# Attention between dense matmuls, loads on another queue, and pooling moved behind the dense stage

## The chip, the cores and the metric

The kernel runs on one core of a Trainium2 chip. The metric is the time of one execution on the device in microseconds (us), as the median of several runs. The core's engines work at the same time, each through its own list of instructions in order: TensorE (PE) multiplies matrices, VectorE (DVE) and ScalarE (ACT) work elementwise, GpSimd (POOL) and SyncE (SP) here mostly issue DMA transfers. An instruction may wait for another engine or for a transfer; what stands behind it on its engine then waits too.

## The reference

One transformer-like block on 2048 positions of width 1024, in float32:

```python
u = _rmsnorm(h, norm_mix_g[l])
z = jnp.einsum('bsd,dn->bsn', u, w_in[l])
q, k, v, pz, ga, gp = jnp.split(z, offs, axis=-1)
a = _attention_branch(q, k, v)                 # 3 groups of 4 heads, dilations 1, 4, 16
p = _pool_branch(pz, w_pool_grp[l], pool_scale[l])   # trailing means over 2, 4, 8, 16
merged = (jax.nn.sigmoid(ga) * jnp.einsum('bsc,cd->bsd', a, w_att_out[l])
          + jax.nn.sigmoid(gp) * jnp.einsum('bsc,cd->bsd', p, w_pool_out[l]))
h = h + jnp.einsum('bsd,de->bse', merged, w_out[l])
m = _rmsnorm(h, norm_mlp_g[l])
hid = jnp.square(jax.nn.relu(jnp.einsum('bsd,df->bsf', m, w_mlp_in[l])))
h = h + jnp.einsum('bsf,fd->bsd', hid, w_mlp_out[l])
return _rmsnorm(h, norm_final_g)
```

Attention looks back over 128 strided positions, softmax with a distance penalty; the three groups' results are weighted by their softmax denominators.

## The kernel before

The sequence is worked on in two halves of 1024 positions (hf 0 and 1), each as two tiles of 512 (t). Positions lie along the free axis, channels on the 128 partitions.

**Normalisation** (normed_x). For each t the eight tiles of x are loaded on SP's queue, squared on ACT, and the squares added on DVE (L277, seven adds per t). A matmul with a matrix of ones (L124, tile xst) sums over the partitions; ACT and DVE make the factor 1/rms from it, DVE multiplies x by it (L285). Seven left-hand combinations of the scaled tiles (B11, T1, T2, B22, T3, B21, T4; combine) are each split into a high and a low part: a cast on ACT (L141), a subtraction on DVE (L142).

**Dense stage** (stage). Per half there are 20 pairs of output blocks: nine for q, k, v, three for the pooling input (pz), eight for the gates (g). Two pairs are worked side by side in each of ten rounds. A pair takes seven steps in the order A11, S1, S2, S4, S3, A12, A22, a block form of multiplication with seven products; each step is 12 matmuls of 128x512 into a PSUM bank with the tag "b" or "c" (L148 to L150). The weights are loaded on SP's queue, summed on DVE (L291 to L294) and split (L141, L142). The results go through DVE or ACT (total, L308 to L312) and are stored from POOL's queue. A half has 1680 of these matmuls.

**Hook.** After each round j a hook issues a share of the half's attention blocks (32 in half 1, 64 in half 2; the share is 5 or 8) and at j = 6, 7, 8 four pooling blocks each. At j = 8 the first half also issues the second half's normalisation and the second half the group weights.

**Attention block** (attention). It loads q, k and v (SP), multiplies q by k for two heads (tiles s0, s1; L458), adds the penalty on DVE (L460), takes the row maximum (L462), the exponentials on ACT (L464), transposes the scores on PE (tile t, L468), copies them (L470), multiplies by v (tile o, L474), copies the result (L476) and stores it from POOL's queue (L477). A block reads one or two blocks of keys.

**Pooling block** (pooling). It loads a 128x528 piece of pz (SP), adds shifted copies on DVE (L422), subtracts the token (L428; L431 and L432 mend the first 16 positions) and stores it to p_d from POOL's queue.

**Group weights** transpose the row maxima and sums (row_s, row_t), form the three groups' weights and store them (wts_d). **merge** loads the pooled tiles (p), the attention results (o) and the weights (wb), combines and splits them, and multiplies by w_pool_out (z_pp) and w_att_out (z_pq); the gates follow. Behind it come w_out (z_o) and the MLP.

Eight PSUM banks are shared out: three "b", two "c", s0, s1, and "t" for transposes, attention results, sums of squares. In SBUF the temporaries tt, hx and h22 have four buffers each: the scores sb and their transposes pt share tt, q and k lie in hx, v and the result in h22.

A scheduler sets the order of the instructions on each engine from the program's order and its own estimate of time, so that neighbours in the code need not be neighbours on an engine.

Of the kernel before, what the change touches and what calls it, by code (L numbers as in the profile page):

```python
# [9 lines left out]
F32 = mybir.dt.float32  # L10
# [7 lines left out]
P = 128  # L18
D = 1024
KD = D // P  # L20
SEQ = 2048
C = 512
# [25 lines left out]
def trunk_kernel(ctx: ExitStack, tc, xt, w_qk, w_v, w_pz, w_grp, w_gates, w_att, w_pool, w_o, w_1, w_2, cols, out):  # L48
    nc = tc.nc
# [71 lines left out]
    def ssq_to_rstd(pool, ps, ssq, dst, key, tags, bufs):  # L121

        n = ssq.shape[-1]
        nc.tensor.matmul(ps, ones, ssq, start=True, stop=True)  # L124
        y = pool.tile([P, C], F32, name=f"y_{key}", tag=tags[0], bufs=bufs)[:, :n]
        nc.scalar.activation(y, ps, AF.Ln, scale=1.0 / D, bias=eps)
        nc.scalar.activation(y, y, AF.Exp, scale=-0.5)
        v = pool.tile([P, C], F32, name=f"var_{key}", tag=tags[1], bufs=bufs)[:, :n]
        nc.vector.tensor_scalar(v, ps, 1.0 / D, EPS, op0=ALU.mult, op1=ALU.add)
        t = pool.tile([P, C], F32, name=f"t_{key}", tag=tags[2], bufs=bufs)[:, :n]  # L130
        nc.vector.tensor_mul(t, y, y)
        nc.vector.tensor_mul(t, t, v)
        nc.vector.tensor_scalar(t, t, -0.5, 1.5, op0=ALU.mult, op1=ALU.add)
        nc.vector.tensor_mul(dst, y, t)
# [18 lines left out]
    psd = pool_of(pds, "psd", space=PSUM)  # L153
    banks = {"pool": psd, "b": 3, "c": 2}

# [41 lines left out]
    wp = pool_of(wps, "wp")  # L197
# [5 lines left out]
    def wtile(name, tag="zz", bufs=ZB):  # L203
        return wp.tile([P, C], F32, name=name, tag=tag, bufs=bufs)
# [51 lines left out]
    def normed_x(hf):  # L256

        got = {}
        ssq = [wtile(f"xss_{hf}_{t}", "ssq", 2) for t in range(2)]

        def load(k, t, tag):
# [3 lines left out]

        for t in range(2):
            for k in range(KD):
                tag = {(0, 0): "tt", (1, 0): "hx", (1, 1): "h22", (0, 1): "zz"}[t, k // KH]
                x = load(k, t, tag)
                if tag != "zz":  # L270
                    got[k, t] = x
                if k == 0:
                    nc.scalar.square(ssq[t], x)
                else:
                    sq = wtile(f"xsq_{hf}_{k}_{t}")
                    nc.scalar.square(sq, x)
                    nc.vector.tensor_add(ssq[t], ssq[t], sq)  # L277
            ps = psd.tile([P, C], F32, name=f"xst_{hf}_{t}", tag="t")
            ssq_to_rstd(wp, ps, ssq[t], ssq[t], f"x{hf}_{t}", ("zz",) * 3, ZB)

        def piece(k, t, tag):
# [4 lines left out]
            return x  # L286
        return combine(piece, f"u{hf}")

# [122 lines left out]
    def pooling(c, n):  # L411

        key = f"{c}_{n}"
        z = temp(f"pz_{key}", "hx", TW)
        nc.sync.dma_start(z, pz_d[n, :, c * C:c * C + TW])
        wmax = max(w for _, _, w in POOL_SEGS[n])
# [18 lines left out]
    def attention(g, r, blk, hp):  # L435
# [4 lines left out]
        own, ks = slice(blk * P, (blk + 1) * P), slice((blk + 1 - nb) * P, (blk + 1) * P)  # L440
        qk = temp(f"qk_{key}", "hx", 3 * P)
        q, k = qk[:, :P], qk[:, P:P + W]
        nc.sync.dma_start(q, qk_d[g][hp, :, r, own])
        nc.sync.dma_start(k, qk_d[g][2 + hp, :, r, ks])
        vo = temp(f"vo_{key}", "h22", 3 * P)
        v, o = vo[:, P:P + W].rearrange("p (b f) -> p b f", b=nb), vo[:, :P]
        nc.sync.dma_start(v, v_d[g].rearrange("(i r) f -> r i f", r=d)[r, ks, hp * P:(hp + 1) * P]
                          .rearrange("(b p) f -> p b f", p=P))
# [17 lines left out]
        for par in range(2):  # L466
            for b in range(nb):
                nc.tensor.transpose(ps_t[:, par, b * P:(b + 1) * P], s[:, par, b * P:(b + 1) * P], ident)  # L468
        pt = temp(f"pt_{key}", "tt").rearrange("p (h j) -> p h j", h=2)[:, :, :W]
        nc.scalar.copy(pt, ps_t[:, :, :W])  # L470
        ps_o = psd.tile([P, C], F32, name=f"o_{key}", tag="t")[:, :P]
        for b in range(nb):
# [40 lines left out]

    next_inputs = [normed_x(0)]
    for hf in range(2):
        order = (1, 0, 2) if hf == 0 else (2, 1, 0)
# [10 lines left out]
        queue = [b for g in order for b in work[g]]  # L527
        share = -(-len(queue) // (7 if hf == 0 else 8))

        def hook(j):  # L530
            if j:
                for _ in range(min(share, len(queue))):
                    attention(*queue.pop(0))
            if j in (6, 7, 8):
                for n in (2 * j - 12, 2 * j - 11):
                    for t in range(2):
                        pooling(2 * hf + t, n)
            if j == 8:
                if hf == 0:
                    next_inputs.append(normed_x(1))  # L540
                else:
                    group_weights()
        stage(pairs, next_inputs[hf], hook)
    pds.close()
# [7 lines left out]
    def merge(hf):  # L552
# [10 lines left out]
        for t in range(2):  # L563
            c = 2 * hf + t
            for hp in range(2):
                a = None
                for g, d in enumerate(DIL):
                    o = temp(f"o_{c}_{g}_{hp}", "hx")
                    nc.sync.dma_start(o.rearrange("p (r i) -> p r i", r=d),
                                      o_d[g][hp, :, :, c * C // d:(c + 1) * C // d])  # L570
                    wb = wtile(f"wb_{c}_{g}_{hp}")
# [303 lines left out]
```

## Time and profile before

| what | value |
|---|---|
| median of 3 runs | 2937.55 us (2935.2 to 2938.49) |
| the profiled execution | 2930.1 us, its span 2928.3 us |
| PE busy | 2647.8 us (90%) |
| DVE busy | 1834.1 us (63%) |
| ACT busy | 1364.7 us (47%) |
| POOL busy | 384.2 us (13%) |
| mean granted PE clock | 0.933 of full speed (2.4 GHz) |

A busy share is an average over stages; the two dense halves with attention take the first 1200 us of the span, the merge follows up to about 1440, then w_out and the MLP. The granted clock stands at one of two levels, 1.2 or 2.4 GHz, and a mean between them says for how much of a stretch each held.

### The profile page before, as it was taken

Reading aid. Unit: us, or ns where it says so; the run is one execution under the profiler, and the core shown is the slowest. Engines: PE = TensorE matmul, PEld = TensorE weight load, DVE = VectorE, ACT = ScalarE, POOL = GpSimd, SP = SyncE. Lnnn points to the kernel's source line nnn. Section 1 sums busy time; section 2 is a strip of 40 time slices with the busy share of each in tenths; the row PEclk is TensorE's granted clock in tenths of the full one; section 3 lists DMA queues with packets and bytes.
Section 4 is the critical chain, followed back from the end, with each engine's and each line's share of the span. In section 5 each row is a group of like instructions: output and inputs, shape, how many; then the busy total and the mean of one; then the engine's idle time right before and its main releaser. Section 6 shows DMA issues by size and latency. Waiting matters only on the chain.

```text
span 2928.3 us, 35991 instructions
## 1 busy us (share of the span) xinstructions
PE 2647.8 (90%) x11838; PEld 2098.6 (72%) x11838; DVE 1834.1 (63%) x3031; ACT 1364.7 (47%) x2651; POOL 384.2 (13%) x667
## 2 busy tenths in 40 slices
PE   4799999289999998687899899989999899999996
PEld 4677777177767774466687688878887788878885
DVE  4854546784444455675798755586665584687557
ACT  3434443343444443332465555565555444464444
POOL 2012111011111111111011221112222000000000
PEclk7899999599989995788999999999999999999998
DMA  5234434243334344598766654445555946683433
GB/s 181 82 120 129 133 111 156 103 128 115 117 95 139 106 152 142 137 252 218 238 223 225 244 182 177 172 142 184 187 187 197 327 119 198 206 267 108 126 112 126
DMA packets 262475, 480.29 MB, mean 164 GB/s; under 512 B 57664, under 2 KB 108704, under 8 KB 262288
## 3 DMA queue, kind: packets, MB, share of 16 engines
q1 hardware_dynamic: 204592, 328.82, 35.9%
q0 software_dynamic: 57696, 149.17, 14.9%
q8 instruction: 93, 1.52, 0.2%
q14 instruction: 94, 0.77, 0.1%
HBM read 326.65 MB, written 151.14 MB: 163 GB/s over the span
## 4 chain that ended last, share of the span: by engine, by line
PE 60%; issue 21%; DVE 7%; DMA 6%; POOL 4%; ACT 1%; SPq 0%; POOLq 0%; DVEq 0%; ACTq 0%
PE z L149 6%; PE z L150 6%; PE z L148 6%; PE z_c_b L148 4%; PE z_c_b L150 4%; PE z_c_b L149 4%; PE z_c_c L150 3%; PE z_c_c L149 3%; PE z_c_c L148 3%; DMA x<-hid_d 1%; PE z_qk_b L148 1%; PE z_qk_b L149 1%; PE z_qk_b L150 1%; PE s L458 1%; PE z_qk_c L149 1%
## 5 line engine op out<-in xcount | busy, mean ns | idle before, releaser
L142 DVE TENSOR_TENSOR wl_S<-r_S,wh_S 128x512 fp32r<-128x512 f32 x128 | 88.3, 690 | 123.5 <-ACT wh_S L141 123.5
L141 ACT CAST wh_S<-r_S 128x512 fp32r<-128x512 f32 x128 | 79.9, 624 | 182.1 <-PE z L149 162.5
L149 PE MATMUL z<-xl_T,wh_S 128*128 128x512 f32 x384 | 149.6, 390 | 2.8 <-DVE xl_T L142 2.8
L150 PE MATMUL z<-xh_T,wl_S 128*128 128x512 f32 x384 | 149.4, 389 | 0.0
L142 DVE TENSOR_TENSOR wl_c_S<-s_c,wh_c_S 128x512 fp32r<-128x512 f32 x128 | 87.8, 689 | 97.4 <-ACT wh_c_S L141 97.1
L148 PE MATMUL z<-xh_T,wh_S 128*128 128x512 f32 x384 | 135.7, 389 | 0.0
L141 ACT CAST wh_c_S<-s_c 128x512 fp32r<-128x512 f32 x128 | 77.5, 619 | 98.0 <-PE z_c_b L149 48.1
L142 DVE TENSOR_TENSOR wl_g_S<-s_g,wh_g_S 128x512 fp32r<-128x512 f32 x64 | 44.2, 692 | 107.0 <-ACT wh_g_S L141 104.4
L141 ACT CAST wh_A<-r_A 128x512 fp32r<-128x512 f32 x96 | 59.6, 621 | 107.9 <-PE z L149 75.9
L464 ACT ACTIVATE sb<-sb,negm 128x256 f32<-128x256 f32 (+1 forms) x192 | 87.3, 458 | 45.0 <-DVE negm L462 44.8
L458 PE MATMUL s<-qk 64*128 64x256 f32 (+1 forms) x384 | 100.3, 442 | 7.9 <-DMA qk<-qk_d 4.7
L142 DVE TENSOR_TENSOR wl_A<-r_A,wh_A 128x512 fp32r<-128x512 f32 x96 | 66.1, 688 | 64.9 <-ACT wh_A L141 64.0
L477 POOL DMA_DIRECT2D o_d<-vo x96 | 52.0, 542 | 403.2 <-ACT vo L476 402.8
L149 PE MATMUL z<-xl_B,wh_A 128*128 128x512 f32 x256 | 101.1, 395 | 0.9 <-DVE xl_B L142 0.9
L148 PE MATMUL z<-xh_B,wh_A 128*128 128x512 f32 x256 | 94.6, 401 | 6.0 <-ACT xh_B L141 6.0
L150 PE MATMUL z<-xh_B,wl_A 128*128 128x512 f32 x256 | 99.9, 393 | 0.0
L460 DVE SCALAR_TENSOR_TENSOR sb<-steps,s 128x256 f32<-128x256 f32 (+1 forms) x192 | 62.8, 358 | 54.1 <-PE s L458 54.0
L470 ACT COPY pt<-t 128x512 f32<-128x512 f32 (+1 forms) x96 | 47.4, 493 | 91.9 <-PE t L468 91.9
L141 ACT CAST wh_c_A<-r_c 128x512 fp32r<-128x512 f32 x96 | 59.5, 620 | 65.1 <-PE z_c_c L149 31.1
L745 POOL TENSOR_TENSOR y<-y,frs 128x256 f32<-128x256 f32 x4 | 3.2, 811 | 656.5 <-ACT fsq L730 648.9
L149 PEld LDWEIGHTS z<-xl_T,wh_S 128*128 128x128 f32 x384 | 72.1, 188 | 18.6 <-DVE xl_T L142 3.7
L150 PEld LDWEIGHTS z<-xh_T,wl_S 128*128 128x128 f32 x384 | 72.1, 188 | 14.9
(659 smaller groups left out, 8490.7 us busy)
## 6 DMA issues: line engine op xcount, KB each, us to landing
x<-hid_d SPq DMA_DIRECT2D x160, 256.0 KB, 4.5
r_c<-in_w SPq DMA_DIRECT2D x64, 512.0 KB, 6.1
r_S<-w2s_d SPq DMA_DIRECT2D x128, 256.0 KB, 2.6
r_A<-in_w SPq DMA_DIRECT2D x96, 256.0 KB, 3.7
r_g<-in_w_gates SPq DMA_DIRECT2D x32, 512.0 KB, 3.9
r_w<-in_w SPq DMA_DIRECT2D x32, 512.0 KB, 3.2
w2s_d<-s_w POOLq DMA_DIRECT2D x64, 256.0 KB, 5.0
hid_d<-zS_c POOLq DMA_DIRECT2D x64, 256.0 KB, 3.6
```

Source lines behind the costliest of these rows:

```text
L141: nc.scalar.copy(hi, src)
L142: nc.vector.tensor_sub(lo, src, hi.bitcast(F32))
L148: nc.tensor.matmul(ps, lh, rh, start=start and i == 0, stop=False, skip_group_check=True)
L149: nc.tensor.matmul(ps, lh, rl, start=False, stop=False, skip_group_check=True)
L150: nc.tensor.matmul(ps, ll, rh, start=False, stop=stop and i == n - 1, skip_group_check=True)
L458: nc.tensor.matmul(ps_s[par], q[rows], k[rows], start=True, stop=True)
L460: nc.vector.scalar_tensor_tensor(s[:, par], steps[:, 2 * P - W:], SLOPES[HPG * g + 2 * hp + par] * d, ps_s[par], op0=ALU.mult, op1=ALU.add)
L464: nc.scalar.activation(s[:, par], s[:, par], AF.Exp, bias=nm[:, par:par + 1], accum_out=ls[:, par:par + 1])
L470: nc.scalar.copy(pt, ps_t[:, :, :W])
L477: nc.gpsimd.dma_start(o_d[g][hp, :, r, own], o)
L745: nc.gpsimd.tensor_mul(y, y, rs)
```

## The change

1. First half's normalisation: the 16 squares are summed by 16 matmuls with ones into the banks s0 and s1, in place of 14 DVE adds and two matmuls.
2. Second half's normalisation: loads and squares are issued at j = 7 (before: 8), the factors at j = 8.
3. PSUM: "b" has two banks (before: three), attention's result a bank "o" of its own.
4. SBUF: q, k and the result share one hx tile (four of them), the scores have tt alone, the transposed scores lie with v in h22.
5. The loads of q, k, v, of pz and of the merge's o are issued from POOL's queue (before: SP's).
6. Shares of 6 and 10 attention blocks per round (before: 5 and 8).
7. First half's pooling at j = 6 and 7, six blocks each; the second half's pooling behind the dense stage.

```diff
-        n = ssq.shape[-1]
-        nc.tensor.matmul(ps, ones, ssq, start=True, stop=True)
+        n = ps.shape[-1]
+        if ssq is not None:
+            nc.tensor.matmul(ps, ones, ssq, start=True, stop=True)
...
-    banks = {"pool": psd, "b": 3, "c": 2}
+    banks = {"pool": psd, "b": 2, "c": 2}
...
         for t in range(2):
+            if hf == 0:
+                ps[t] = psd.tile([P, C], F32, name=f"xst_{hf}_{t}", tag=f"s{t}")
             for k in range(KD):
...
-                if k == 0:
+                if k == 0 and hf:
                     nc.scalar.square(ssq[t], x)
                 else:
                     sq = wtile(f"xsq_{hf}_{k}_{t}")
                     nc.scalar.square(sq, x)
-                    nc.vector.tensor_add(ssq[t], ssq[t], sq)
-            ps = psd.tile([P, C], F32, name=f"xst_{hf}_{t}", tag="t")
-            ssq_to_rstd(wp, ps, ssq[t], ssq[t], f"x{hf}_{t}", ("zz",) * 3, ZB)
+                    if hf:
+                        nc.vector.tensor_add(ssq[t], ssq[t], sq)
+                    else:
+                        nc.tensor.matmul(ps[t], ones, sq, start=k == 0, stop=k == KD - 1)
+
+        def factors():
+            for t in range(2):
+                if hf:
+                    ps[t] = psd.tile([P, C], F32, name=f"xst_{hf}_{t}", tag="t")
+                ssq_to_rstd(wp, ps[t], ssq[t] if hf else None, ssq[t], f"x{hf}_{t}", ("zz",) * 3, ZB)
...
-        nc.sync.dma_start(z, pz_d[n, :, c * C:c * C + TW])
+        nc.gpsimd.dma_start(z, pz_d[n, :, c * C:c * C + TW])
...
-        qk = temp(f"qk_{key}", "hx", 3 * P)
-        q, k = qk[:, :P], qk[:, P:P + W]
-        nc.sync.dma_start(q, qk_d[g][hp, :, r, own])
-        nc.sync.dma_start(k, qk_d[g][2 + hp, :, r, ks])
-        vo = temp(f"vo_{key}", "h22", 3 * P)
-        v, o = vo[:, P:P + W].rearrange("p (b f) -> p b f", b=nb), vo[:, :P]
-        nc.sync.dma_start(v, v_d[g].rearrange("(i r) f -> r i f", r=d)[r, ks, hp * P:(hp + 1) * P]
+        qko = temp(f"qko_{key}", "hx", 4 * P)
+        o, q, k = qko[:, :P], qko[:, P:2 * P], qko[:, 2 * P:2 * P + W]
+        nc.gpsimd.dma_start(q, qk_d[g][hp, :, r, own])
+        nc.gpsimd.dma_start(k, qk_d[g][2 + hp, :, r, ks])
+        v = temp(f"v_{key}", "h22", W).rearrange("p (b f) -> p b f", b=nb)
+        nc.gpsimd.dma_start(v, v_d[g].rearrange("(i r) f -> r i f", r=d)[r, ks, hp * P:(hp + 1) * P]
...
-        pt = temp(f"pt_{key}", "tt").rearrange("p (h j) -> p h j", h=2)[:, :, :W]
+        pt = temp(f"pt_{key}", "h22").rearrange("p (h j) -> p h j", h=2)[:, :, :W]
...
-        ps_o = psd.tile([P, C], F32, name=f"o_{key}", tag="t")[:, :P]
+        ps_o = psd.tile([P, C], F32, name=f"o_{key}", tag="o")[:, :P]
...
-        share = -(-len(queue) // (7 if hf == 0 else 8))
+        share = -(-len(queue) // (6 if hf == 0 else 7))
...
-            if j in (6, 7, 8):
-                for n in (2 * j - 12, 2 * j - 11):
-                    for t in range(2):
-                        pooling(2 * hf + t, n)
-            if j == 8:
-                if hf == 0:
+            if hf == 0:
+                if j in (6, 7):
+                    for n in range(3 * (j - 6), 3 * (j - 5)):
+                        for t in range(2):
+                            pooling(t, n)
+                if j == 7:
                     next_inputs.append(normed_x(1))
-                else:
-                    group_weights()
-        stage(pairs, next_inputs[hf], hook)
+                if j == 8:
+                    next_inputs[1][0]()
+            elif j == 8:
+                group_weights()
+        stage(pairs, next_inputs[hf][1], hook)
+    for n in range(6):
+        for t in range(2):
+            pooling(2 + t, n)
...
-                    nc.sync.dma_start(o.rearrange("p (r i) -> p r i", r=d),
-                                      o_d[g][hp, :, :, c * C // d:(c + 1) * C // d])
+                    nc.gpsimd.dma_start(o.rearrange("p (r i) -> p r i", r=d),
+                                        o_d[g][hp, :, :, c * C // d:(c + 1) * C // d])
```

What this does to the order of the instructions is seen at three places. A name like z_g1_7_b0 is the bank "b" of gate pair 7 in half 2, o_0_0_15_1 an attention result (group, residue class, block, pair of heads), xst_1_0 the sum of squares of half 2's first tile; the last number only counts tiles.

PE where half 2's dense work ends, before: behind the last gate matmul attention goes on by itself.

```order
L148 MATMUL z_g1_7_b0_9425<-mT4h_u1_3_5027,wh_g1_7_A22_9643 128x512
L149 MATMUL z_g1_7_b0_9425<-mT4l_u1_3_5028,wh_g1_7_A22_9643 128x512
L150 MATMUL z_g1_7_b0_9425<-mT4h_u1_3_5027,wl_g1_7_A22_9644 128x512
L474 MATMUL o_1_2_3_0_8033<-pt_1_2_3_0_8031,vo_1_2_3_0_8014 64x128 x4
L458 MATMUL s0_1_3_3_0_8074<-qk_1_3_3_0_8069 128x256
L458 MATMUL s1_1_3_3_0_8075<-qk_1_3_3_0_8069 128x256
L468 MATMUL t_1_2_3_1_8055<-ident_95,sb_1_2_3_1_8047 128x128 x4
L458 MATMUL s0_1_3_3_1_8103<-qk_1_3_3_1_8098 128x256
L474 MATMUL o_1_2_3_1_8062<-pt_1_2_3_1_8060,vo_1_2_3_1_8043 64x128 x4
L458 MATMUL s1_1_3_3_1_8104<-qk_1_3_3_1_8098 128x256
```

From here on no dense matmul of half 2 is left; some 20 blocks follow, each waiting only for its own chain and its neighbours'.

The same engine in the changed kernel, at its last attention block and behind its last gate matmul: the block stands between dense matmuls of gate pair 6, and the merge's z_pp follows the last gate matmul directly.

```order
L152 MATMUL z_g1_6_b0_9280<-mB11h_u1_0_4654,wl_g1_6_A11_9277 128x512
L150 MATMUL z_g1_6_b0_9280<-mB11h_u1_1_4659,wh_g1_6_A11_9276 128x512
L470 MATMUL s0_0_0_15_1_8853<-qko_0_0_15_1_8848 128x256
L151 MATMUL z_g1_6_b0_9280<-mB11l_u1_1_4660,wh_g1_6_A11_9276 128x512
L470 MATMUL s1_0_0_15_1_8854<-qko_0_0_15_1_8848 128x256
L152 MATMUL z_g1_6_b0_9280<-mB11h_u1_1_4659,wl_g1_6_A11_9277 128x512
L150 MATMUL z_g1_6_b0_9280<-mB11h_u1_2_4664,wh_g1_6_A11_9276 128x512
L486 MATMUL o_0_0_14_1_8812<-pt_0_0_14_1_8810,v_0_0_14_1_8793 64x128 x4
```

```order
L152 MATMUL z_g1_7_b0_9299<-mT4h_u1_2_5024,wl_g1_7_A22_9518 128x512
L150 MATMUL z_g1_7_b0_9299<-mT4h_u1_3_5029,wh_g1_7_A22_9517 128x512
L151 MATMUL z_g1_7_b0_9299<-mT4l_u1_3_5030,wh_g1_7_A22_9517 128x512
L152 MATMUL z_g1_7_b0_9299<-mT4h_u1_3_5029,wl_g1_7_A22_9518 128x512
L150 MATMUL z_pp_0_0_0_9847<-mB11h_pa_0_0_9671,wh_p0_0_0_9827 128x512
L151 MATMUL z_pp_0_0_0_9847<-mB11l_pa_0_0_9672,wh_p0_0_0_9827 128x512
```

The attention rows have moved up by some 170 rows, ahead of the rest of the gates' work.

PE at the change of halves, before (xst are half 2's sums of squares, z_g0 the gates of half 1):

```order
L150 MATMUL z_g0_7_c1_4428<-mT1h_u0_3_507,wl_g0_7_S1_4425 128x512
L468 MATMUL t_0_0_7_1_3839<-ident_95,sb_0_0_7_1_3831 128x128 x4
L474 MATMUL o_0_0_7_1_3846<-pt_0_0_7_1_3844,vo_0_0_7_1_3827 64x128 x4
L124 MATMUL xst_1_0_4281<-xss_1_0_4241,ones_100 128x512
L124 MATMUL xst_1_1_4331<-xss_1_1_4242,ones_100 128x512
L148 MATMUL z_g0_6_b0_4371<-mT2h_u0_0_551,wh_g0_6_S2_4443 128x512
```

The two sums stand one behind the other, in front of the third step (S2, with mT2) of gate pair 6.

The same engine and place in the changed kernel:

```order
L150 MATMUL z_g0_5_c1_4122<-mT1h_u0_3_509,wh_g0_5_S1_4118 128x512
L151 MATMUL z_g0_5_c1_4122<-mT1l_u0_3_510,wh_g0_5_S1_4118 128x512
L152 MATMUL z_g0_5_c1_4122<-mT1h_u0_3_509,wl_g0_5_S1_4119 128x512
L126 MATMUL xst_1_0_4321<-xss_1_0_3959,ones_100 128x512
L150 MATMUL z_g0_4_b0_4065<-mT2h_u0_0_553,wh_g0_4_S2_4137 128x512
L151 MATMUL z_g0_4_b0_4065<-mT2l_u0_0_554,wh_g0_4_S2_4137 128x512
```

The first sum has moved to the same step of gate pair 4, two pairs earlier; the second stands 152 rows on, inside gate pair 7.

ACT at the same place, in the changed kernel (xsq are half 2's squares, the COPY rows free the banks of gate pairs 4 and 5):

```order
L282 ACTIVATE xsq_1_5_1_4024<-xh22_1_5_1_4022 128x512
L282 ACTIVATE xsq_1_6_1_4029<-xh22_1_6_1_4027 128x512
L282 ACTIVATE xsq_1_7_1_4034<-xh22_1_7_1_4032 128x512
L321 COPY zA11_g0_4_4078<-z_g0_4_b0_4065 128x512
L321 COPY zA11_g0_5_4097<-z_g0_5_b0_4084 128x512
L321 COPY zS1_g0_4_4116<-z_g0_4_c1_4103 128x512
L321 COPY zS1_g0_5_4135<-z_g0_5_c1_4122 128x512
```

All 16 squares have moved ahead of these copies, which the third step on PE waits for.

DVE at the start of the merge, before (pf_3_5 is the last pooling block, mB11l_pa the first low part of a pooled tile for z_pp):

```order
L428 SCALAR_TENSOR_TENSOR pf_3_5_9284<-sum_3_5_8_9282,pz_3_5_9274 128x512
L498 COPY rowt_0_9299<-row_t_0_9294 16x512
L498 COPY rows0_1_9306<-row_s0_1_9301 16x4x128
L501 TENSOR_TENSOR row_min_9357<-rows0_0_9292,rows0_1_9306 16x512
L498 COPY rowt_1_9313<-row_t_1_9308 16x4x128
L498 COPY rows0_2_9334<-row_s0_2_9315 16x16x32
L142 TENSOR_TENSOR mB11l_pa_0_0_9670<-p_0_0_9667,mB11h_pa_0_0_9669 128x512
```

The same engine in the changed kernel (L435 and L441 are the pooling's lines there):

```order
L441 SCALAR_TENSOR_TENSOR pf_3_4_9634<-sum_3_4_4_9630,pz_3_4_9624 64x512
L435 TENSOR_TENSOR sum_2_5_1_9640<-pz_2_5_9638 128x527
L441 SCALAR_TENSOR_TENSOR pf_3_4_9634<-sum_3_4_8_9632,pz_3_4_9624 64x512
L144 TENSOR_TENSOR mB11l_pa_0_0_9672<-p_0_0_9669,mB11h_pa_0_0_9671 128x512
L435 TENSOR_TENSOR sum_2_5_2_9642<-sum_2_5_1_9640 128x525
L435 TENSOR_TENSOR sum_2_5_4_9644<-sum_2_5_2_9642 128x521
L435 TENSOR_TENSOR sum_2_5_8_9646<-sum_2_5_4_9644 128x513
L435 TENSOR_TENSOR sum_3_5_1_9653<-pz_3_5_9651 128x527
```

The pooling of half 2, which stood beside the last attention blocks, has moved behind the last dense total and around the first splits of the merge.

## Rows read from the trace of the kernel before

**Rows 1.** windows: busy us (xcount) of PE, PEld, DVE, ACT, POOL; PEclk, DMA, GB/s

```profile
100.00:150.00 50.00, 50.00 (x225) 41.39 (x223) 36.16 (x56) 21.38 (x38) 6.26 (x10) 1.00 0.37 117
500.00:550.00 50.00, 14.45 (x77) 10.66 (x75) 34.29 (x63) 10.66 (x24) 5.94 (x11) 0.68 0.51 180
550.00:600.00 50.00, 28.15 (x103) 20.76 (x104) 39.34 (x65) 30.24 (x49) 1.62 (x3) 0.71 0.13 38
```

**Rows 2.** PE's timeline, front: start us, us, engine, line, ... [idle before]

```profile
70.74 1.02 PE L124 MATMUL xst<-xss,ones 128*128 128x512 f32 x2
89.37 0.79 PE L149 MATMUL z_qk_c<-mT1l_u,wh_qk_S 128*128 128x512 f32 x1 [2.95 <-DVE mT1l_u L142]
```

**Rows 3.** change of halves: timelines of PE and DVE, one chain row

```profile
514.47 0.66 PE L474 MATMUL o<-pt,vo 128*64 128x128 f32 x8 [0.68 <-ACT pt L470]
553.06 2.08 PE L124 MATMUL xst<-xss,ones 128*128 128x512 f32 x2 [37.94 <-DVE xss L277]
569.40 2.08 PE L124 MATMUL xst<-xss,ones 128*128 128x512 f32 x2 [14.26 <-DVE xss L277]
576.00 0.80 PE L148 MATMUL z_g_b<-mT2h_u,wh_g_S 128*128 128x512 f32 x1 [4.53 <-ACT zA_g L308]
...
513.92 0.70 DVE L422 TENSOR_TENSOR sum<-pz 128x527 f32<-128x527 f32 x1
538.09 0.69 DVE L428 SCALAR_TENSOR_TENSOR pf<-sum,pz 128x512 f32<-128x512 f32 x1
...
539.08 6.14 DMA p_d<-pf
```

**Rows 4.** PE's timeline, end of half 2 to first w_out matmul

```profile
1095.70 0.40 PE L150 MATMUL z_g_b<-mT4h_u,wl_g_A 128*128 128x512 f32 x1
...
1117.79 1.11 PE L468 MATMUL t<-ident,sb 128*128 128x128 f32 x4
...
1204.28 0.52 PE L148 MATMUL z_pp<-mB11h_pa,wh_p 128*128 128x512 f32 x1
...
1260.16 0.39 PE L148 MATMUL z_pq<-mB22h_pa,wh_a 128*128 128x512 f32 x1
...
1438.67 0.39 PE L148 MATMUL z_o_b<-mB11h_o,wh_o_A 128*128 128x512 f32 x1
```

**Rows 5.** PE's timeline: an attention block inside dense work

```profile
970.35 0.66 PE L474 MATMUL o<-pt,vo 128*64 128x128 f32 x8
970.93 0.70 PE L458 MATMUL s<-qk 64*128 64x256 f32 x4
...
975.35 0.60 PE L468 MATMUL t<-ident,sb 128*128 128x128 f32 x4
```

**Rows 6.** groups by line: busy us, mean ns, idle before, releasers

```profile
L277 DVE TENSOR_TENSOR xss<-xss,xsq 128x512 f32<-128x512 f32 x28 | 19.3, 688 | 14.3 <-ACT xsq L276 13.8
L460 DVE SCALAR_TENSOR_TENSOR sb<-steps,s 128x256 f32<-128x256 f32 (+1 forms) x192 | 62.8, 358 | 54.1 <-PE s L458 54.0
L462 DVE TENSOR_REDUCE negm<-sb 128x2 f32<-128x512 f32 (+1 forms) x96 | 54.4, 567 | 2.2
...
L464 ACT ACTIVATE sb<-sb,negm 128x256 f32<-128x256 f32 (+1 forms) x192 | 87.3, 458 | 45.0 <-DVE negm L462 44.8
L476 ACT COPY vo<-o 128x128 f32<-128x128 f32 x96 | 25.4, 265 | 82.6 <-PE o L474 81.0 <-DMA o_d<-vo 0.8
```

**Rows 7.** the merge's window with the most traffic, as rows 1

```profile
1300.00:1350.00 50.00, 41.06 (x179) 32.96 (x177) 24.78 (x39) 18.79 (x33) 12.07 (x18) 0.94 1.05 284
```

**Rows 8.** DMA issues: KB each, us to landing; POOL's o stores

```profile
qk<-qk_d SPq DMA_DIRECT2D x138, 64.0 KB, 2.1
qk<-qk_d SPq DMA_DIRECT2D x54, 128.0 KB, 2.6
...
o_d<-vo POOLq DMA_DIRECT2D x96, 64.0 KB, 2.3
...
L477 POOL DMA_DIRECT2D o_d<-vo x96 | 52.0, 542 | 403.2 <-ACT vo L476 402.8 <-issue 0.2
```

More of the change, by code (lines that the diff above doesn't have):

```diff
@@ L259, in normed_x @@
         ssq = [wtile(f"xss_{hf}_{t}", "ssq", 2) for t in range(2)]
+        ps = {}
         def load(k, t, tag):
@@ L286, in piece @@
             return x
-        return combine(piece, f"u{hf}")
+        return factors, combine(piece, f"u{hf}")
     def sums(a11, a12, a21, a22, key):
@@ L514, in trunk_kernel @@
     next_inputs = [normed_x(0)]
+    next_inputs[0][0]()
     for hf in range(2):
```

## Prediction

> **What bounds the kernel now.** I read the table of 50-us windows first. In most of the two dense halves TensorE (PE) is busy all the time at a granted clock of 1.00, 225 instructions in 50 us, 0.222 us each [rows 1]. More buffers or shorter chains gain nothing there. Time is lost where a window holds fewer: 77 and 103 around the change of halves (500 to 600 us) [rows 1], and again from 1100 to 1200 us. Then I read PE's timeline at these places, and the order of the changed kernel for the same ones.
>
> At the **change of halves** PE stops after an attention result at 514.47 (0.66 long) and takes up dense work at 576.00; between stand two 2.08 us sums of squares. It waits 37.94 + 14.26 + 4.53 = 56.7 us [rows 3]. The releaser named is the add of squares, but behind it lies a chain: VectorE (DVE) pools from 513.9 to 538.8, then the store of a pooled block takes 6.14 us to land, only then does a tile come free for a load of x, then come squares and adds [rows 3].
>
> At the **tail** the last dense matmul of half 2 stands at 1095.70 and the merge's first (z_pp) at 1204.28 [rows 4]: 108 us with 20 attention blocks and the group weights, at half clock (4 transposes 1.11 us, against 0.60 inside dense work) [rows 4, 5].
>
> **Front.** The first half's 14 adds of squares leave DVE (14 x 0.688 = 9.6 us [rows 6]) and PE gets 16 ones-matmuls in place of two. One (two records) costs 1.02 us at full clock [rows 2] and 2.08 at half [rows 3], so they are 16 to 33 us of PE, put into the time before its first dense matmul, where it waits for loads and squares. What gains is the second sum: it comes at 70.74, behind the first 24 dense matmuls, and the next step's dense work, which needs the factor made from it, goes on at 89.37 [rows 2]. In the new order both sums stand ahead of all dense work, and DVE has 14 adds less in its row. If the sums run at full clock, the second factor is there about 10 us earlier; at half clock the first dense matmul slips by some 4 us and the step still comes 3 earlier. I take 7 (3 to 10).
>
> **Change of halves.** The new order puts the loads and squares a step of the schedule earlier, so PE stops behind the S1 step of gate pairs 4 and 5 rather than 6 and 7, and two things still stand ahead of it on the other engines. ScalarE (ACT) has all 16 squares ahead of the copies that free PE's "b" banks, and the last x loads again wait for the last pooling store. But more pooling is done by then: 22 pooling operations come behind the last split PE still needs, where 47 took 24.9 us (513.92 to 538.8 [rows 3]), so 22 x 0.53 = 11.7. From pooling's end to the first sum took 553.06 - 538.8 = 14.3 us in the old kernel, store, load and squares included [rows 3]. Seven more squares and two copies on ACT add about 9 x 0.55 = 5. The hole is 11.7 + 14.3 + 5 = 31 in place of 56.7: gain **26**. If the loads don't wait for that store, only 11.7 plus 14 adds (8.5 to 9.6) plus a copy remain, 22, and the gain is 35; if pooling keeps all of its 24.9, the hole is 44 and the gain 12.
>
> **Tail.** Shares of 6 and 10 blocks per step let all 64 blocks of half 2 stand between dense matmuls; the last result (o_0_0_15_1) has over 100 dense matmuls behind it, and the row transposes of the group weights stand there too. The 20 blocks of the tail then cost PE what a block costs inside dense work at full clock: results 0.66, scores 0.70, transposes 0.60 as listed, 1.96, each overlapping what follows by some 0.08 (970.35 to 970.93 is 0.58) [rows 5], so 1.7; 20 x 1.7 = 34, plus 3 for the row transposes. So dense work ends 37 later, counted from 1096.0. Behind it, DVE now has half 2's pooling. Its order has 33 pooling operations between the last dense total and the first split for the merge, 33 x 0.53 to 0.70 = 17 to 23 us; about 5 of it passes beside the last 24 dense matmuls. z_pp starts some 15 later. From z_pp to the first w_out matmul (z_o) it is 1438.67 - 1204.28 = 234.4 us [rows 4]; 56 of that pass before z_pq (1260.16), which needs the group weights' stores and loads; these now come ahead, so I take 225. Then 15 + 225 = 240 stands in place of 1438.67 - 1096.0 = 342.7: gain 342.7 - 37 - 240 = **66** (52 with the whole 234.4 and 20 before z_pp, 78 with z_pq 10 earlier).
>
> **What is added.** Pooling beside the merge brings 12 loads (128 x 528) and 12 stores (128 x 512), 6.2 MB in all, into a stage that at its fullest moves 284 GB/s with a DMA share of 1.05 [rows 7]: 0 if they pass before that stretch, 22 if they lengthen it; most of them stand ahead of it, so I take 8. "b" has two banks in place of three and a block's scores stand some 22 dense matmuls ahead of its transposes, where 54 stood. The chain between is two DVE operations of 0.36, a reduction of 0.57 and two exponentials of 0.46, 2.2 us by the means [rows 6] and some 2.8 for a block of two, against 22 x 0.222 = 4.9. DVE's and ACT's queues may eat the 2 us between, now and then. No row shows either; bounds 0 (a copy hides behind the other bank) and 30 (96 blocks x 0.3), and I take 8, nearer to the rows with covered chains. Attention's own result bank and the fourth score tile cost nothing. Tiles that hold q, k and o until the store has landed cost nothing if the loop below has room. Clusters of blocks without dense work between stay (8 in the old order near 860 us, 8 in the new): nothing.
>
> **Sum:** 7 + 26 + 66 - 8 - 8 = 83. The profiled run's 2930.1 becomes 2847; that execution lies 7.45 under the median of the runs, 2937.55, which becomes 2854.5, say **2855**.
>
> **Rivals.**
> *The loop on GpSimd's queue (slower).* q, k, v loads (288), pooling's and the merge's loads move from SyncE's queue to that of GpSimd (POOL), which works in order: behind a q load that waits for the o store of four blocks ago stand the dense stores and the next v load. The four tiles make a loop: copy 0.27, issue 0.54, store 2.3, two issues 1.1, load 2.6, scores 0.7, 5.1 to the transposes, 0.6, 20 dense matmuls 4.4, result 0.7: 18.3 us [rows 6, 8]. Four blocks take PE 4 x (18.7 x 0.222 + 1.4) = 22, so 3.7 us of POOL waits are free, and each further one costs a quarter per block. With 9 us of waits the loop is 27.3, 1.3 per block, 90 blocks 119 us: 2855 + 119 = **2974**. It turns the sign from 7.4 us of waits on. For it: POOL waits some 2.3 us for landing in each block, and stores are issued between. Against it: issues are 0.54 us, four or five a block of 5.5. Chance 0.10.
> Here a rule speaks against the move. A 64 KB store from POOL lands 2.3 us after issue, a 64 KB q or k load from SyncE 2.1 [rows 8], with DVE at work beside both: no row shows a DMA held up by DVE. The Trainium skill (SBUF — State Buffer, Who interferes with whom) says that a VectorE copy, cast or tensor_scalar in a two-port mode shuts GpSimd out of its port, and that two-input forms contend with its reads, so that its DMAs wait for descriptors. If by that rule each of three issues in the loop waited for one DVE operation (0.69), the loop would be 20.4, still under 22, and the time the forecast's; the room left would be 1.6, and the chance of this rival rather 0.15. The rows don't bear it out.
> *The hole keeps its length.* The x loads wait for the pooling store as before, and the squares now hold up ACT's bank copies too. Gain 0 in place of 26: **2881**. Chance 0.13.
> *The merge takes it back.* The full 22 of transfers, and z_pp to z_o at 234.4 with 20 before z_pp: 2855 + 14 + 14 = **2883**. Chance 0.12.
> *Transposes wait.* 64 blocks x 0.6 because DVE's queue makes the chain longer than 4.9: 2855 + 38 = **2893**. It also stands for the order not doing what is meant: blocks between dense work, yet PE waiting. Chance 0.12.
>
> **How the numbers follow.** Forecast 0.45 (2815 to 2895 by its bounds), better than its bounds 0.04, the three middling rivals 0.37, two of them together, near no change, 0.04, slower loop 0.10. Faster by over 0.2% (some 6 us, what a measurement can tell): 0.86; same 0.03; slower 0.11. The range, 2805 to 2910, leaves out the slower loop and the pairs of rivals.
>
> **What would show it.** Right: dense work of half 2 without a window under 200 instructions in 50 us, z_pp within 25 us of the last dense matmul, one hole of 25 to 35 us between the halves, the first S1 step near 82. Wrong: PE waiting at transposes for ACT, or at scores for a q or k load (the loop), z_o more than 255 behind the last dense matmul (merge), a hole of over 45 between the halves.

## The result, and the profile after

| | before | after |
|---|---|---|
| median of the runs, us | 2937.31 (4 runs) | 2854.01 (4 runs, 2850.68 to 2859.61) |
| ratio, 95% interval | | 0.9719 [0.9700, 0.9739] |
| profiled execution, us (span) | 2930.1 (2928.3) | 2859.6 (2857.8) |
| first S1 step's second dense part (z_qk_c), us | 89.37 | 81.15 |
| PE's waits at the change of halves, us | 56.7 | 32.7 at the first sum, 5.25 at the second |
| last dense matmul of half 2 ends | 1096.1 | 1118.0 |
| first merge matmul (z_pp) | 1204.28 | 1155.44 |
| first w_out matmul (z_o) | 1438.67 | 1369.69 |

The forecast was 2855 us, the medians say 2854, a gain of 83.3. The two profiled executions say 70.5, because the one of after is the longest of its four runs (5.6 above their median) and that of before lies 7.2 under its own. Places in the program are compared by the profiled ones, so 70 is what the terms below have to explain; the other 12 to 13 us are the spread of single runs, and no place can be given for them.

Windows of the changed kernel, 50 us each; columns as in [rows 1]:

```profile
450.00:500.00 50.00, 17.49 (x71) 12.96 (x69) 38.69 (x68) 14.76 (x26) 8.61 (x16) 0.68 0.55 191
500.00:550.00 50.00, 44.57 (x177) 35.93 (x178) 30.59 (x49) 23.69 (x38) 4.34 (x8) 0.91 0.24 85
...
800.00:850.00 50.00, 42.49 (x206) 27.94 (x205) 22.43 (x52) 20.94 (x74) 24.10 (x46) 0.79 0.33 105
...
1050.00:1100.00 50.00, 50.00 (x317) 37.09 (x316) 32.98 (x55) 21.89 (x51) 15.33 (x27) 1.00 0.36 117
1100.00:1150.00 50.00, 18.00 (x80) 14.58 (x78) 32.86 (x49) 5.00 (x9) 22.15 (x37) 0.73 0.76 224
```

The hole between the halves [rows 1, 3] has moved from 500–600 to 450–500 and is shorter; a short second one stands where the second sum's factor is taken up. From 600 on no window of half 2's dense work has under 200 PE instructions; up to its last matmul at 1118 PE stops only in short stretches. PE's timeline of the same kernel (start, duration, engine and line, idle before with its releaser) at the places of [rows 2 to 4]:

```profile
81.15 0.80 PE L151 MATMUL z_qk_c<-mT1l_u,wh_qk_S 128*128 128x512 f32 x1 [4.15 <-DVE mT1l_u L144]
...
497.17 2.04 PE L126 MATMUL xst<-xss,ones 128*128 128x512 f32 x2 [31.72 <-DVE xss L284]
500.18 0.79 PE L150 MATMUL z_g_b<-mT2h_u,wh_g_S 128*128 128x512 f32 x1 [0.97 <-ACT zA_g L321]
...
547.00 0.80 PE L150 MATMUL z_g_b<-mT2h_u,wh_g_S 128*128 128x512 f32 x1 [5.25 <-ACT zA_g L321]
...
1117.62 0.39 PE L152 MATMUL z_g_b<-mT4h_u,wl_g_A 128*128 128x512 f32 x1
...
1155.44 0.80 PE L150 MATMUL z_pp<-mB11h_pa,wh_p 128*128 128x512 f32 x1 [37.44 <-ACT mB11h_pa L143]
...
1369.69 0.39 PE L150 MATMUL z_o_b<-mB11h_o,wh_o_A 128*128 128x512 f32 x1
```

Two long waits are left on PE, 31.7 us at the first sum of squares and 37.4 before the merge. PE's list of waits (us in total, times, longest) shows the same, and that attention hardly waits for a load or an exponential:

```profile
PE z_pp L150 <- ACT mB11h_pa L143: 39.7, 3, 37.4
PE xst L126 <- DVE xss L284: 31.7, 1, 31.7
...
PE t L480 <- ACT sb L476: 5.5, 6, 1.6
...
PE s L470 <- DMA qko<-qk_d: 0.8, 2, 0.4
```

What holds z_pp is in the queues. First SyncE (SP), then POOL, then DVE, in the stretch before it:

```profile
1109.71 6.07 SPq L602 DMA_DIRECT2D r_p<-in_w_pool  x3
1151.82 9.96 SPq L579 DMA_DIRECT2D p<-p_d  x6
```

```profile
1128.63 0.55 POOL L428 DMA_DIRECT2D pz<-pz_d  x1 [4.34 <-DMA wb<-wts_d]
...
1141.00 0.82 POOL L590 DMA_DIRECT2D wb<-wts_d  x1 [2.35 <-DMA wb<-wts_d]
```

```profile
1136.28 0.71 DVE L435 TENSOR_TENSOR sum<-pz 128x527 f32<-128x527 f32 x1 [10.48 <-DMA pz<-pz_d]
...
1144.21 0.71 DVE L435 TENSOR_TENSOR sum<-pz 128x527 f32<-128x527 f32 x1 [5.03 <-DMA pz<-pz_d]
```

SP's first load of a pooled block for the merge (p, L579) is issued only at 1151.82, 36 us after the load ahead of it. It needs an "hx" tile, and those are held by pooling's inputs (pz), whose own loads land late among those of the group weights (wb).

### The profile page after: what moved, and what is told of

Same layout as the page of the kernel before. It is cut to its first block, busy times and chain, and to the rows that moved or that the text cites. A ratio compares the mean times of both kernels' runs of the same rounds, so it can differ in the third digit from the quotient of the medians.

```text
span 2857.8 us, 35938 instructions
## 1 busy us (share of the span) xinstructions
PE 2631.2 (92%) x11866; PEld 2076.3 (73%) x11866; DVE 1821.3 (64%) x3017; ACT 1359.6 (48%) x2649; POOL 583.9 (20%) x1003
## 4 chain that ended last, share of the span: by engine, by line
PE 77%; DVE 8%; DMA 8%; issue 4%; ACT 2%; POOL 1%; SPq 0%; DVEq 0%; ACTq 0%; POOLq 0%
PE z L151 7%; PE z L150 7%; PE z L152 7%; PE z_c_b L150 4%; PE z_c_b L152 4%; PE z_c_b L151 4%; PE z_c_c L152 3%; PE z_c_c L150 3%; PE z_c_c L151 3%; PE s L470 2%; PE z_qk_b L151 2%; PE z_qk_b L152 2%; PE z_qk_b L150 2%; PE z_g_b L151 2%; PE z_g_b L150 2%
## 5 line engine op out<-in xcount | busy, mean ns | idle before, releaser
L699 POOL DMA_DIRECT2D w2s_d<-s_w x64 | 34.7, 542 | 359.4 <-DVE s_w L304 350.2
L459 POOL DMA_DIRECT2D v<-v_d x96 | 61.9, 644 | 114.4 <-ACT qko L488 69.6
L150 PEld LDWEIGHTS z<-xh_T,wh_S 128*128 128x128 f32 x384 | 72.1, 188 | 15.1
```

Of the source, the lines that this page charges most:

```text
L150: nc.tensor.matmul(ps, lh, rh, start=start and i == 0, stop=False, skip_group_check=True)
L459: nc.gpsimd.dma_start(v, v_d[g].rearrange("(i r) f -> r i f", r=d)[r, ks, hp * P:(hp + 1) * P] .rearrange("(b p) f -> p b f", p=P))
L699: nc.gpsimd.dma_start(w2s_d[i][j], s)
```

## Experiments

Each kernel is the changed one with the edit shown. A ratio is always against the kernel before. The changed kernel run once more beside the first of them gave 2856.76 us, 0.9723 [0.9707, 0.9739], and a gain or loss below is counted from there. Where the intervals of two ratios overlap, a difference of a few us is not shown by the times alone.

**1. Change of halves: squares and pooling back to their old rounds.**

```diff
-                if j in (6, 7):
-                    for n in range(3 * (j - 6), 3 * (j - 5)):
+                if j in (6, 7, 8):
+                    for n in (2 * j - 12, 2 * j - 11):
...
-                if j == 7:
-                    next_inputs.append(normed_x(1))
                 if j == 8:
+                    next_inputs.append(normed_x(1))
                     next_inputs[1][0]()
```

> Undoes the change at the half: squares and loads of half 2 again at j = 8, pooling of half 1 at j = 6, 7 and 8. By my sum this is worth 24 us (hole 32.7 in place of 56.7): 2878 us, PE waiting some 50 to 60 us between the halves. Rival: the shorter hole comes from the loads that left SyncE's queue or from the three banks, not from the places in the code; then 2854 within 6.

Measured: 2837.43, 0.9665 [0.9646, 0.9684]. Undoing the part to which I gave a gain of 26 us makes the kernel 19 us faster. Which half of the edit does it was the next question.

**2. Only the x loads and squares back at j = 8, pooling left at 6 and 7** (the last three lines of that diff).

> Half 2's squares and loads go back to j = 8 and nothing else; pooling of half 1 stays at j = 6 and 7. Undoing both had made the kernel 17 us faster, with no PE wait over 7 us between the halves. Theory N: the early squares are the cost (16 squares ahead of the copies that free the banks of gate pairs 4 and 5, and the first sum in front of their third step): about 2837, waits of some 10 us between the halves. Rival P: the pooling's places are the cost (12 blocks in two steps rather than three): 2854 within 5, PE waiting about 30 us.

Measured: 2836.09, 0.9651 [0.9636, 0.9667]. The early squares alone cost about 20 us. PE's timeline of this kernel between the halves:

```profile
508.58 1.43 PE L126 MATMUL xst<-xss,ones 128*128 128x512 f32 x2 [3.76 <-DVE xss L284]
...
516.23 2.08 PE L126 MATMUL xst<-xss,ones 128*128 128x512 f32 x2 [6.22 <-DVE xss L284]
...
522.52 0.80 PE L150 MATMUL z_g_b<-mT2h_u,wh_g_S 128*128 128x512 f32 x1 [4.21 <-ACT zA_g L321]
```

Three waits of 14.2 us together stand where the changed kernel waits 32.7 and, at the second sum, 5.25: 23.7 less, of which 2.9 come back as a wait for a gate weight. That covers the 20. The loads of x start no later here, as SP's queue shows (changed kernel first, then this one):

```profile
472.96 2.95 SPq L267 DMA_DIRECT2D xhx<-in_xt  x2
```

```profile
471.48 3.54 SPq L267 DMA_DIRECT2D xhx<-in_xt  x2
```

The first load stays where it was, and the last of the sixteen comes at 489.9 in the changed kernel, 501.0 here. So a round earlier in the code brought the first sum 11 us sooner (497.17, 508.58), but put it where PE runs out of other work at 465 rather than at 505. With the squares a round later, PE has the dense work of that round to do while ACT squares and DVE adds. That leaves the question why before lost 56.7 us there, with the squares in the same round. The trace of before shows it in SP's own queue. Below it stand the longest wait in that stretch, from SP's list of waits, and the line of pooling's loads in the changed kernel (first and last start):

```profile
494.34 29.75 SPq L415 DMA_DIRECT2D pz<-pz_d  x8
529.92 0.33 SPq L263 DMA_DIRECT2D xhx<-in_xt  x1
```

```profile
SPq L415 <- DVE pf L428: 16.8, 2, 16.1
```

```profile
L428 POOL DMA_DIRECT2D pz<-pz_d x12: 539/544/544, 408.4 to 465.7; - x12
```

Before, eight of pooling's twelve loads were issued from 494 to 524, one of them after a wait of 16.1 us for a tile that an earlier pooling block still held, and the x loads stood behind them. DVE took up that pooling again at 513.92 [rows 3], beside the half's last attention result at 514.47. In the changed kernel that result stands at 431.89, with the old shares (experiment 8) at 473.80; that the loads follow it is suggested by this and not shown. Pooling's loads are all issued by 466 in the changed kernel, and in every variant run here by 480, with the loads on SP (462.4 in experiment 4) and with the old shares (479.2 in experiment 8) too. So neither the queue nor the shares alone explain it, and neither does pooling's place (465.0 in experiment 1). What is left is how soon attention lets tiles go: q, k and o share one tile, the transposed scores have moved to another pool tag, four score tiles are in flight, and attention's result has a PSUM bank of its own. These were not run one by one.

**3. Both score banks as one tile of two banks.**

```diff
-        ps_s = [psd.tile([P, C], F32, name=f"s{par}_{key}", tag=f"s{par}")[:, :W] for par in range(2)]
+        ps_2 = psd.tile([P, 2, C], F32, name=f"s_{key}", tag="s")
+        ps_s = [ps_2[:, par, :W] for par in range(2)]
```

The tile also serves the sums of the first half and the group weights' transposes. It aims at a thing that I had not foreseen. In the changed kernel the score matmuls of a block's two heads are sometimes parted by other work (first piece), elsewhere adjacent (second):

```profile
963.37 0.70 PE L470 MATMUL s<-qko 64*128 64x256 f32 x2
964.00 0.50 PE L150 MATMUL z_g_c<-mT1h_u,wh_g_S 128*128 128x512 f32 x1
964.34 0.40 PE L151 MATMUL z_g_c<-mT1l_u,wh_g_S 128*128 128x512 f32 x1
964.66 0.70 PE L470 MATMUL s<-qko 64*128 64x256 f32 x2
965.29 0.66 PE L486 MATMUL o<-pt,v 128*64 128x128 f32 x8
...
976.84 0.70 PE L470 MATMUL s<-qko 64*128 64x256 f32 x4
977.47 0.50 PE L152 MATMUL z_g_b<-mT2h_u,wl_g_S 128*128 128x512 f32 x1
```

Parted, each head takes 0.63 us to the next start (963.37 to 964.00, 964.66 to 965.29); adjacent, both take 0.63 together. Of 96 blocks 25 are parted, counted by runs of score records on PE; in the kernel before 36 are.

> The two heads' scores of a block lie in one PSUM tile of two banks, so that their two matmuls wait for the same release and stand together on PE. Theory S (split scores): in the changed kernel 25 of 96 blocks have other matmuls between the two score matmuls, and each split costs PE 0.63 us and some 0.1 for the next matmul, since two adjacent score matmuls take as long as one; 25 x 0.72 = 18 us less, 2836 us, all of it before the last dense matmul of half 2. Rival W (waits): the second half of the dense stage is longer than foreseen because PE waits for chains; then joining the two banks gains nothing and waiting for both may cost: 2854 to 2865 us, dense end of half 2 unchanged or later.

Measured: 2850.01, 0.9702 [0.9688, 0.9717], 6.7 us less than the changed kernel, a third of what was expected. The edit did not join all pairs: by the same count 16 blocks are still parted here, nine fewer, and 9 x 0.72 = 6.5. The score lines of the two kernels (busy us, mean ns; changed kernel first) agree:

```profile
L470 PE MATMUL s<-qko 64*128 64x256 f32 (+1 forms) x384 | 77.3, 393 | 0.8 <-DMA qko<-qk_d 0.8
```

```profile
L473 PE MATMUL s<-qko 64*128 64x256 f32 (+1 forms) x384 | 70.0, 391 | 1.0 <-DMA qko<-qk_d 1.0
```

77.3 - 70.0 = 7.3 us. Dense work of half 2 ends at 1106.7 in place of 1118.0, and z_o comes at 1358.3, 11.4 earlier.

**4. Pooling's loads back on SP's queue.** One line: `nc.gpsimd.dma_start(z, pz_d[...])` becomes `nc.sync.dma_start(z, pz_d[...])`.

> Only the pooling's loads of pz go back to SyncE's queue. Theory Q (queue order): PE's 37 us hole before z_pp comes from pz loads that stand behind the group weights' stores and wb loads on GpSimd's queue; without that DVE pools without its waits of 10.5 and 5.0 us, the hole is some 22 us and the time some 12 to 15 less: 2840 us. Rival T (traffic): the loads are late because DMA engines are full with the wb loads (landing 12.9 us); then they land late from SyncE as well, the hole stays above 32 us and the time within 5 of 2854.

Measured: 2855.74, 0.9720 [0.9706, 0.9734], no difference. The chain of waits of this kernel before the merge:

```profile
1122.39 10.27 DMA pz<-pz_d
...
1133.76 9.79 DMA p_d<-pf
```

The load still takes 10.27 us to land, and z_pp stands 34.6 behind dense work, so POOL's queue is not what makes it late. That the traffic around it does, with six loads of group weights on their way, is argued and not shown by itself. The Trainium skill (DMA: Bandwidth & Descriptors, Issuing engines are not separate DMA queues) says that DMAs started by different engines run on the same 16 DMA engines and interleave; this row agrees, since from another queue the load lands no sooner.

**5. Both edits together** (3 and 4).

> Both edits together. If S and Q hold and act at different places: 18 + 13 less, 2823 us. If only one holds, its part alone: 2836 or 2840. If the merge's gates or weights are late next, less than the sum.

Measured: 2845.69, 0.9689 [0.9676, 0.9703]. That is 4.3 under experiment 3, but the intervals overlap and z_o stands at 1358.0 as it did there: whether the queue adds to it stays open.

**6. The merge's loads of pooled blocks in a tile of their own.**

```diff
-                x = temp(f"p_{c}_{n}", "hx")
+                x = wtile(f"p_{c}_{n}", "s", SB)
```

> Only the merge's pooled tiles p lie in the five buffers of the tag s (free once half 2's last weight sums are used) in place of hx, whose four buffers the pooling of half 2 takes first. Theory B (buffers): PE's hole before z_pp (37 us) is the wait for hx, since p of half 1 was stored long before; z_pp then follows the last dense matmul within 10 us and the kernel is 15 to 30 us faster, 2825 to 2840. Rival C (chain of the merge): z_pq, which needs the attention results o and the weights wb, stays where it is (about 70 us behind the last dense matmul), z_pp only waits later, and the time falls by less than 6 us.

Measured: 2861.03, 0.9741 [0.9726, 0.9756], 4 us slower, within the intervals, and no gain. PE's timeline of this kernel at the merge's start:

```profile
1114.57 0.39 PE L152 MATMUL z_g_b<-mT4h_u,wl_g_A 128*128 128x512 f32 x1
1114.80 0.39 PE L150 MATMUL z_pp<-mB11h_pa,wh_p 128*128 128x512 f32 x1
...
1179.34 0.80 PE L150 MATMUL z_pq<-mB22h_pa,wh_a 128*128 128x512 f32 x1 [48.06 <-ACT mB22h_pa L143]
...
1373.44 0.39 PE L150 MATMUL z_o_b<-mB11h_o,wh_o_A 128*128 128x512 f32 x1
```

z_pp follows the dense work without any wait: the "hx" tiles were the cause of the 37.4 us. But PE then waits 48.06 before z_pq. That comes 9.7 earlier than in the changed kernel (1189.06), and z_o still 4 later: PE waits 22.7 for the later pieces' weights and gates, 12.9 in the changed kernel. What the merge needs last is not its pooled part; whether the loss comes from the "s" buffers, which hold weight sums too, was not tried. With experiment 3 on top the time was 2856.1, 0.9724 [0.9707, 0.9741], 6 above experiment 3 alone, so taking that wait away gains nothing there either.

**7. Loads of q, k and v back on SP's queue**, against the rival of the loop: three `nc.gpsimd.dma_start` become `nc.sync.dma_start`.

> Only q, k and v loads go back to SyncE's queue. Theory L (the loop has room): the four tiles' loop needs some 18 us and has 22, so GpSimd's queue costs nothing: 2854 within 5. Rival G (GpSimd's queue): loads wait behind stores on it and PE pays in places; then 8 to 20 us faster than 2854. Rival H: on SyncE the loads wait behind the weights' loads; slower by 5 or more.

Measured: 2852.14, 0.9707 [0.9690, 0.9724], at most a few us better, within the intervals. The loop on POOL's queue has room.

**8. Shares of blocks back to one more round.** `(6 if hf == 0 else 7)` becomes `(7 if hf == 0 else 8)`.

> Only the shares go back to 5 and 8 attention blocks per round. Theory A (shares): they are what puts the 20 blocks of the tail between dense matmuls; then the tail returns, 40 us or more slower, 2895 and above. Rival F (four score tiles, result bank): a block leaves its tiles sooner and the scheduler fits all 64 in at either share; then 2854 within 10, the last dense matmul of half 2 no earlier and no tail of attention behind it.

Measured: 2876.91, 0.9793 [0.9776, 0.9809], 20 us slower, between what the theories expected. PE's waits in this kernel at the two holes:

```profile
509.16 2.05 PE L126 MATMUL xst<-xss,ones 128*128 128x512 f32 x2 [34.24 <-DVE xss L284]
...
1170.94 0.80 PE L150 MATMUL z_pp<-mB11h_pa,wh_p 128*128 128x512 f32 x1 [52.09 <-ACT mB11h_pa L143]
```

The hole between the halves hardly changes; the one before the merge grows by 14.7. Yet no tail of attention blocks came back behind the dense work, so the shares alone are not what put the 20 blocks of before among dense matmuls.

**9. Half 2's pooling back in its rounds** (j = 6, 7, 8, as in the kernel before).

> Half 2's pooling goes back into the rounds j = 6, 7, 8. Theory D (DVE and buffers at the merge): PE's hole of 37 us before z_pp falls to under 15, and the end of the merge comes 10 to 20 us earlier, 2835 to 2845. Rival E (the merge is bound behind z_pp by the weights wb, by o and by DMA traffic, as p in the tag s showed): the hole falls but z_pq and the end stay, 2854 within 6. Rival X: pooling in the dense stage takes DVE time and tiles that attention needs there, slower by over 6.

Measured: 2863.17, 0.9747 [0.9727, 0.9768], 6 us slower, with intervals that overlap. PE's waits in this kernel:

```profile
PE z_pq L150 <- ACT mB22h_pa L143: 18.1, 2, 13.5
PE row_s L500 <- DVE rows L510: 15.7, 1, 15.7
```

The hole before z_pp is gone and z_pp comes at 1133.6, 22 earlier, but PE waits at the group weights' transposes and before z_pq instead, and z_o stands at 1375.9, 6 later. Pooling beside the merge costs nothing against its old place, and may gain these few us.

**10. The parts that gained, together:** squares back at j = 8 (2), one tile for both score banks (3), pooling's loads on SP (4).

> Three edits on the changed kernel: the second half's x loads and squares come a step later again (after gate pair 8), a block's two score tiles lie in one PSUM tile of two banks, and the pooled tiles' loads in the merge go back to SyncE's queue. Apart, the first gave 2836.1 and the other two together 2845.7, beside some 2856.8 for the changed kernel. If the two gains are independent (theory I: the first is PE's wait between the halves, the second PE's time in the split blocks of half 2 and what follows it), 2856.8 - 20.7 - 11.1 = 2825. If the merge's start holds the end whatever PE saves before it (theory M: the pooled tiles and the blocks of p that wait for them decide, and already hold 36.9 us of PE in the first run), the second edit gives at most the 4 us that the pooled tiles' loads gave apart: about 2832 to 2836, with the wait before z_pp grown to 43 or more and dense work of half 2 ending some 10 us earlier than in the first run.

Measured: 2825.56 us (5 runs), 0.9626 [0.9609, 0.9643] of before's 2934.93 (9 runs). PE's timeline:

```profile
1080.65 0.39 PE L152 MATMUL z_g_b<-mT4h_u,wl_g_A 128*128 128x512 f32 x1
1122.77 0.79 PE L150 MATMUL z_pp<-mB11h_pa,wh_p 128*128 128x512 f32 x1 [41.73 <-ACT mB11h_pa L143]
...
1331.97 0.39 PE L150 MATMUL z_o_b<-mB11h_o,wh_o_A 128*128 128x512 f32 x1
```

The gains add. z_o is 37.7 earlier than in the changed kernel. From the end of dense work to z_o it takes 251 us here, 251.7 in the changed kernel and in experiment 3, and 245.7 in 2: what is saved before the merge reaches the end nearly whole. The 37 to 42 us of idle PE at the merge's start are still there, but experiment 6 shows that ending the wait before z_pp alone does not win them.

## Why the prediction was right, and where its steps were not

**Front: right.** The step goes on at 81.15, 8.2 earlier; 7 was put, "near 82" named.

**Change of halves: near in size, wrong in cause.** The hole was put at 31 and is 32.7, with 5.25 more at the second sum, where the copy of a bank is late; half 2 is entered 21.8 earlier beyond the front's gain, where 26 was put. But the step said that the squares' earlier place shortens it. Experiment 2 shows the opposite: that place costs 20, and without it the waits are 14.2. The step that failed is the one that took before's wait to be fixed to the place of the squares. It took the whole chain to move a round forward; the first load of x stayed (472.96 and 471.48), the first sum moved by 11, and PE stops some 40 sooner. It read the releaser, the adds and the pooling on DVE [rows 3], but not SP's queue, where eight pooling loads took 29.75 us to issue for want of tiles. The change let the last of these go 58 us sooner (45 with the old shares), by other parts of it than the one I credited; which, is not shown. That the size came out near is luck. I had also not asked what dense work PE would lose as cover when squares move forward a round.

**Tail: right in kind, too large.** All blocks went between dense matmuls, and the transposes of the group weights too. Three sizes are to be compared.

First, dense work of half 2 was to end 37 later by itself, 45 with the allowance for shorter covers. Counted by the 600th matmul of one kind, half 2 is entered 30.0 earlier than before, and it ends 21.9 later: 51.9. The price of a block held. Between these two points the changed kernel has 256 score records, before 184, at four a block 18 blocks more; counted from one PE record's start to the next, without waits, attention takes 32.0 us more, 1.8 a block where 1.7 was put. PE's waits grow from 4.5 to 11.0, near the 8 allowed. What the sum left out is the dense matmuls: they take 9.9 more in all. A score matmul or an attention result follows one of them 95 times in place of 40, and one so followed takes 0.32 to the next start (964.34 to 964.66, experiment 3), among its own kind 0.222 [rows 1]; 55 x 0.1 is some 5 of it, and the rest is not told apart. Parted scores don't explain the difference: in this stretch before parts 16 blocks, the changed kernel 15.

Second, z_pp was to stand 15 behind dense work and stands 37.4 behind. I counted DVE's 33 pooling operations, and left out that the pooled blocks wait for pooling's tiles, and these for loads that land after some 10 us. Third, from the end of dense work to z_o I put 240, plus 8 for the traffic; 251.7 is measured, against 342.6 before. The late z_pp seems not to have lengthened this: without it PE waited at z_pq (experiment 6).

Together the tail gives 69.0 - 30.0 = 39.0 at z_o, where 66 less the allowances was put, some 50. With the old shares (experiment 8) z_o is still 50.7 earlier than before, the entry to half 2 18.5: a tail gain of 32.2. So of the 39.0 only 7 hang on the shares, to which I gave the blocks' whole move; which other part moved them is not shown.

**Rivals.** The loop on POOL's queue fell: PE waited 0.8 us for q and k in all, and experiment 7 moves the time by at most 5. No row shows a load held up by DVE: q and k land in 2.2 and 2.8 us from POOL's queue, in 2.1 and 2.6 from SP's [rows 8]. Transposes waited 5.5 us, not 38. The hole that keeps its length fell in size, 32.7, though its thought, that the squares' new place gains nothing, was nearer to the cause than my forecast. The merge taking back half came true in part: z_o 251.7 behind dense work is just under the 255 that was named as the sign.

**Sum.** By the profiled executions the gain is 70.5 rather than 83; the medians agree with 83 because of where the two profiled executions lie among the runs. The terms reach z_o at 69.0: 8.2, 21.8 and 39.0, where 7, 26 and 50 were put. So the forecast's closeness to the median is in part luck. Two bounds of the prediction were added up wrongly: the tail's 52 and 78 should be 51 and 76, and its own lower bounds (3 + 12 + 52 - 22 - 30 = 15) reach up to 2922, not 2895.

## What to carry to other kernels

When a releaser names a compute engine, follow the loads behind it back to the queue that issues them: a load that waits for a tile holds every load behind it, and placing the work that waits a round earlier in the code brought its first load no sooner here; ask what holds the tile. Before moving a preparation step earlier, ask what dense work stood beside it and whether the waiting engine loses that as cover; here a round earlier cost 20 us. And where a wait is taken away at the start of a stage, look at what the stage needs last: with the wait before z_pp gone, PE waited for z_pq.

## What the runs showed of the hardware

Two matmuls that each use 64 of the 128 rows take 0.63 us together when they are adjacent in PE's order, and 0.63 each when others stand between them. The Trainium skill (TensorEngine Tiling (Array Packing), Tiling Modes) says that such row tiles work independently and in parallel; the row at 976.84 agrees, and the rows at 963.37 and 964.66 show what is lost when an order parts them. I had also not expected a load of 264 KB to take over 10 us to land at the merge's start, against a median of 3.9 for all 24 of them in the changed kernel (10.27, experiment 4). And attention work between dense matmuls makes its neighbours dearer: the two dense matmuls between the score matmuls at 963.37 and 964.66 take 0.34 and 0.32 us to the next start, not 0.222.
